# Key heads with decays from stored running sums, block transposes on all 128 rows, and an output projection that takes both parts of its input side by side

## The chip, the cores and the metric

The kernel runs on one core of one Trainium2 chip. The core has five engines with an instruction stream each: TensorE (PE in the profile; its weight loads are PEld), VectorE (DVE), ScalarE (ACT), GpSimd (POOL) and SyncE (SP, which here only issues DMAs). The metric is the device time of one launch in microseconds, lower is better. A comparison of two kernels gives the ratio of their times.

## The reference

The program is a trunk of two layers over 256 latent and 256 context tokens with 2048 features, everything in fp32. Layer 0 joins neighbourhood attention and latent attention; layer 1 is a gated DeltaNet in both directions of time; a final RMSNorm ends it. The change lies almost wholly in layer 1. There are 16 key heads, each of which serves two of 32 value heads, chunks of 64 tokens, and two directions with their own log decays `g` and gains `beta`:

```python
def gated_delta_chunked(q, k, v, g, beta, state0):
    gf = jnp.cumsum(gf, axis=-1)                    # within a chunk of 64
    diff = gf[..., :, None] - gf[..., None, :]
    decay = jnp.where(lower, jnp.exp(jnp.where(lower, diff, 0.0)), 0.0)
    kb = kf * bf[..., None]
    lmat = jnp.where(strict, jnp.einsum('bhncd,bhnsd->bhncs', kb, kf) * decay, 0.0)
    rhs = jnp.concatenate([vf * bf[..., None], kb * jnp.exp(gf)[..., None]], axis=-1)
    sol = lax.linalg.triangular_solve(lmat + jnp.eye(CHUNK), rhs, left_side=True, lower=True)
    intra = jnp.where(lower, jnp.einsum('bhncd,bhnsd->bhncs', qf, kf) * decay, 0.0)
    ...
    state, o = lax.scan(step, state0, xs)           # over the chunks, state 128x128

def deltanet_out(o, z, o_norm, w_out):
    o = rmsnorm(o.transpose(0, 2, 1, 3), o_norm)
    return (o.reshape(b, t_len, DN_MIX_WIDTH) * jax.nn.silu(z)) @ w_out
```

For each chunk, direction and value head there is thus a 64x64 table of decays (exponentials of differences of running sums), a lower triangular system with that table times the products of keys, and a table of query-key products times the decays. `w_out` is 4096 x 2048.

## The kernel before, in words

**Matmuls in three parts.** TensorE multiplies a rounded fp32 format, so each weight tile of 128x1024 is loaded (`raw`, L71, 4 buffers), rounded by ACT into `whi` (L77) and the remainder taken by DVE as `wlo` (L78, 3 buffers each). The activations are split alike into `hh` and `hl`. `dense` (L85 to L93) issues three matmuls for each 128 rows of the weight: `whi`·`hh` (L90), `whi`·`hl` (L91), `wlo`·`hh` (L92), with 512 columns for all tokens and 256 for the latent ones alone. `mm_tile` gives their PSUM tile, of which there are two. The projections of layer 1 to keys, queries, values and gates take their input from such a pair; before it, in layer 0, the same two buffers (tags `hh` and `hl`) hold `ch` with `qr`, and then `gh` with `gl`, the parts of the gated attention output.

**Key heads.** `head(kh)` (L679) runs 16 times. It projects K and Q, convolves them over time on DVE with SiLU on ACT (L557 to L580), transposes the keys on PE to `ptk` (L689), and writes keys and queries into `sp`. Then it makes the decays (L716 to L725) in three goes: forward for all four pairs of chunks, backward for all four, and backward once more, transposed, for two. In each, GpSimd multiplies the decays `ghl` of each token by a mask `incl` into `rhs` (L720, once for the rounded part, once for the remainder), PE sums with a triangular matrix `seg` (L722) into the PSUM tile `pd`, and ACT takes the exponential into `DT`. Four by four small matmuls make the products `kk` of keys with keys and with queries (L736). DVE writes `NT` (decay times key products, L744) and, through a masked copy `QKm` (L740), `AT` (decay times query products, L746). `sp` is stored to DRAM in `spk` and `spt`.

**Inverses.** `inverse(sg)` (L752) runs eight times, each for two key heads, and inverts the triangular 64x64 blocks, 64 of them side by side. Their 32x32 diagonal blocks are gathered by a block transpose into `L` (L764, one for each half of the 128 rows, since the block lies in columns 0 to 31 of the upper half's rows and in 32 to 63 of the lower's). Thirty-one steps of forward substitution follow, two DVE instructions each (L778 `outer`, L780 `X`). GpSimd scales `X` (L782; the last time DVE does). Four block transposes on 64 rows write `X` and its transpose into `U` (L785, L787). Then PE makes the off-diagonal block with small matmuls (`px` L798, `pu` L815), ACT copies it into `U` (L819), and `by_chunk` (L587) stores `U` with eight DMAs from SP. The PSUM tiles `pd`, `px` and `pu` share the tag `xu`.

**What sets the order.** `woven` writes the heads three pieces at a time, each head's first pieces ahead of the last of the one before. The first two heads come alone. Then 42 turns each write seven pieces of an inverse, one of a head, and now and then one of `zunits` (L826, the gates of one head). The 42 turns hold heads 2 to 15 and inverses 0 to 6. Behind them, inverse 7 is written among the last gates and the values of head 0. Up to here, what each engine does in which order is worked out ahead from that text by the builder's scheduler and its own cost estimates; at run time each engine goes through its list in order and waits on semaphores. SP has one list of DMAs: a DMA that waits, for instance for its buffer to be read, holds up those behind it.

**Loop and end.** From L1167 on, an order written out by hand for PE, DVE and ACT runs the recurrence over 64 chunk steps, with value projections between them and, when those are used up, `early` (L1151), which does the first 24 of 32 weight blocks of eight output tiles. `gate` (L1135) splits the gated outputs into `gh` and `gl`, which lie where `hh` and `hl` were. Behind the loop, L1264 to L1271 do the rest of the output projection: eight tiles with 8 blocks and eight with 32, 256 columns each. `project` (L613) adds a tile to the residual stream in two halves. The final norm and the stores end the program.

Of the kernel before, what the change touches and what calls it, by code (L numbers as in the profile page):

```python
# [26 lines left out]
def trunk_kernel(ctx: ExitStack, tc: tile.TileContext, g):  # L27
# [57 lines left out]
    def dense(ps, w, off, kt, xh, xl, k0=0, sl=slice(0, T), first=True, last=True):  # L85
# [7 lines left out]
        return end.ins  # L93

# [136 lines left out]
    hh = big.tile([128, KT, T], F32R, name="hh", tag="hh")  # L231
    hl = big.tile([128, KT, T], F32R, name="hl", tag="hl")
# [69 lines left out]
    with tc.tile_pool(name="ab", bufs=2, reuse_waits="tile") as tp, \  # L302
# [142 lines left out]
        ch = big.tile([128, KT, T], F32R, name="ch", tag="hh")  # L445
        qr = big.tile([128, KT, T], F32R, name="qr", tag="hl")
# [33 lines left out]
        gh = big.tile([128, KT, T], F32R, name="gh", tag="hh")  # L480
        gl = big.tile([128, KT, T], F32R, name="gl", tag="hl")
# [24 lines left out]
        hh = big.tile([128, KT, T], F32R, name="hh", tag="hh")  # L506
        hl = big.tile([128, KT, T], F32R, name="hl", tag="hl")
# [18 lines left out]
    incl = dcst("incl", [128, 3, 64], g["dnc"][:, 1152:1344].rearrange("p (a n) -> p a n", a=3))  # L526
    seg = dnp.tile([128, 3, 128], F32R, name="seg", tag="seg")
# [11 lines left out]
    god = scratch("god", [128, 28, S])  # L539

# [72 lines left out]
    def project(u, p):  # L613

        for t in range(2):
            x = x_of[u].rearrange("p (c i) -> p c i", c=4)[:, pair(t)]
            V.scalar_tensor_tensor(x, p[:, t * 128:t * 128 + 128].rearrange("p (h i) -> p h i", h=2),
                                   mods[1][:, 32 + u, 0:1], x, op0=ALU.mult, op1=ALU.add)


    with tc.tile_pool(name="dn", bufs=2, reuse_waits="tile") as tp, \
# [10 lines left out]
        ch = tp.tile([128, 1792], F32, name="cumh", tag="sp", bufs=1)[:, :1152].rearrange("p (a n) -> p a n", a=9)  # L632
        nc.sync.dma_start(ch, g["dnc"][:, 0:1152].rearrange("p (a n) -> p a n", a=9))
        cum, rest, hones = ch[:, 0:2], ch[:, 2:4], ch[:, 4:6]
        A.copy(seg, ch[:, 6:9])
# [25 lines left out]
        ghl = [tp.tile([128, 2, 128], F32R, name=f"ghl{i}", tag=f"ghl{i}", bufs=1) for i in range(2)]  # L661
        A.copy(ghl[0], gfl)
        V.tensor_tensor(ghl[1], gfl, ghl[0].bitcast(F32), op=ALU.subtract)
# [15 lines left out]
        def head(kh):  # L679
# [4 lines left out]
            yield  # L684

# [29 lines left out]
            for d, c, n in ((0, 0, 4), (1, 2, 4), (1, 1, 2)):  # L715
                pd = ps.tile([128, 512], F32, name="pd", tag="xu")[:, :128 * n]  # L716
                for i in range(2):
                    rhs = tp.tile([128, 8, 64], F32R, name="rhs", tag="rhs")[:, :2 * n]
# [33 lines left out]
        def inverse(sg):  # L752
# [68 lines left out]
            for d in range(2):  # L821
                by_chunk(spu[sg][:, d], U[:, d, 16 * d:16 * d + 16])
# [565 lines left out]
```

## Time and profile before

| | |
|---|---|
| time, median of 3 runs | 2547.64 us (2542.07 to 2549.25) |
| profiled execution, its time | 2550.65 us |
| profiled execution, span of the core | 2548.9 us |
| mean granted clock of TensorE | 0.985 |
| bytes moved by DMA | 394.30 MB, mean 155 GB/s |
| share of the chain that ended last | PE 74%, DVE 12%, issue 6%, DMA 4%, ACT 3% |

The trace falls into stretches: 

| us from the start | what runs there | PE busy | DVE busy | granted clock |
|---|---|---|---|---|
| 0 to 800 | modulation, projections and attention of layer 0 | 770.99 | 481.29 | 1.00 |
| 800 to 1100 | output projection of layer 0, modulation of layer 1 | 293.46 | 226.20 | 0.98 |
| 1100 to 1160 | start of layer 1, first key heads | 54.27 | 32.70 | 1.00 |
| 1160 to 1660 | key heads with inverses 0 to 6 | 460.69 | 479.45 | 0.96 |
| 1660 to 1760 | last gates, inverse 7, values of head 0 | 93.77 | 87.87 | 0.95 |
| 1760 to 2430 | loop over the chunks, `early` towards its end | 667.17 | 482.13 | 1.00 |
| 2430 to 2549 | output projection and final norm | 108 | 64 | 1.00 until 2540 |

All numbers but the first row come from one execution that the hardware profiler took. In the rows of a profile, `L778 DVE SCALAR_TENSOR_TENSOR outer<-L,bv,X 128x255` is an instruction of line 778 on DVE that writes tile `outer` from `L`, `bv` and `X`, 128 partitions by 255 elements; `x201` counts such instructions. Busy time of PE includes stretches in which the clock is throttled: the granted clock says to what share.

### The profile page before, as it was taken

How to read it: one execution, taken by the hardware profiler on the slowest of the kernel's cores; microseconds unless marked ns; L12 is line 12 of the kernel's file. 1: busy time of each engine (PE TensorE's matmuls, PEld its weight loads, DVE VectorE, ACT ScalarE, POOL GpSimd, SP SyncE). 2: the span in 40 equal slices, each digit the busy share in tenths (PEclk: the TensorE clock that was granted, in tenths of full speed). 3: DMA queues.
4: the chain of work that ended last, by engine and by line, in shares of the span. 5: the costliest groups of instructions: out<-in, count | busy, mean ns of one | idle time of the engine just before them, and what ended most of it. 6: DMA issues, size and time to landing. Idle time of an engine off the chain costs nothing.

```text
span 2548.9 us, 43398 instructions
## 1 busy us (share of the span) xinstructions
PE 2448.6 (96%) x16586; PEld 2002.5 (79%) x16586; DVE 1853.5 (73%) x3547; ACT 1140.4 (45%) x2468; POOL 275.6 (11%) x261
## 2 busy tenths in 40 slices
PE   6999999999999999999999989899999999999998
PEld 4557888888768778768888888797777777778898
DVE  4644788873456688758999999997777777777654
ACT  4223323233344422377656665543444444445443
POOL 0000000000000000033322332300000000003000
PEclk9999999999999999999999999999999999999999
DMA  8872645532253367645454544573233333335454
GB/s 251 285 267 83 199 163 172 180 127 91 71 198 112 112 216 225 222 155 160 140 167 148 172 145 156 163 211 104 87 107 110 113 103 105 112 93 180 152 188 141
DMA packets 201809, 394.30 MB, mean 155 GB/s; under 512 B 68224, under 2 KB 109696, under 8 KB 201472
## 3 DMA queue, kind: packets, MB, share of 16 engines
q1 hardware_dynamic: 200448, 389.98, 48.7%
q8 instruction: 131, 2.15, 0.3%
q10 hardware_dynamic: 1152, 1.54, 0.2%
q14 instruction: 78, 0.64, 0.1%
HBM read 356.28 MB, written 35.13 MB: 154 GB/s over the span
## 4 chain that ended last, share of the span: by engine, by line
PE 74%; DVE 12%; issue 6%; DMA 4%; ACT 3%; POOL 0%; SPq 0%; DVEq 0%; POOLq 0%; ACTq 0%
PE mm L90 19%; PE mm L91 17%; PE mm L92 17%; PE pks L993 3%; PE pmod L127 3%; DVE wlo L78 3%; PE ptr L1005 2%; DVE acc L566 2%; PE sp L348 2%; DVE outer L778 1%; PE po L348 1%; DVE X L780 1%; DMA mraw<-dn_wm 1%; DVE U L787 1%; PE ptr L1038 1%
## 5 line engine op out<-in xcount | busy, mean ns | idle before, releaser
L90 PE MATMUL mm<-hh,whi 128*128 128x512 f32 (+1 forms) x2784 | 987.0, 355 | 2.4 <-ACT t L643 2.3
L92 PE MATMUL mm<-hh,wlo 128*128 128x512 f32 (+1 forms) x2784 | 959.3, 345 | 12.2 <-DVE wlo L78 11.5
L91 PE MATMUL mm<-hl,whi 128*128 128x512 f32 (+1 forms) x2784 | 959.7, 345 | 0.0
L77 ACT CAST whi<-raw 128x1024 fp32r<-128x1024 f32 (+2 forms) x346 | 337.6, 980 | 650.5 <-PE mm L91 521.4
L90 PEld LDWEIGHTS mm<-hh,whi 128*128 128x128 f32 x2784 | 534.1, 192 | 112.6 <-issue 33.3
L92 PEld LDWEIGHTS mm<-hh,wlo 128*128 128x128 f32 x2784 | 533.2, 192 | 77.1 <-DVE wlo L78 13.1
L91 PEld LDWEIGHTS mm<-hl,whi 128*128 128x128 f32 x2784 | 534.4, 192 | 62.5 <-issue 9.7
L78 DVE TENSOR_TENSOR wlo<-raw,whi 128x1024 fp32r<-128x1024 f32 (+2 forms) x346 | 400.6, 1160 | 204.0 <-ACT whi L77 201.4
L163 DVE SCALAR_TENSOR_TENSOR lacc<-mraw,cond,lacc 128x512 f32<-128x512 f32 x300 | 208.3, 744 | 0.0
L566 DVE SCALAR_TENSOR_TENSOR acc<-cin,taps,acc 128x508 f32<-128x508 f32 (+3 forms) x256 | 191.9, 750 | 7.6 <-ACT acc L557 5.2
L1015 DVE SCALAR_TENSOR_TENSOR vl<-ptr,egm,vh 128x128 fp32r<-128x128 f32 x224 | 64.6, 346 | 98.2 <-ACT rf L1012 39.3
L720 POOL TENSOR_TENSOR rhs<-ghl,incl 128x512 fp32r<-128x512 f32 (+1 forms) x96 | 113.1, 1193 | 186.6 <-PE pd L722 165.9
L778 DVE SCALAR_TENSOR_TENSOR outer<-L,bv,X 128x31 f32<-128x31 f32 (+15 forms) x248 | 118.1, 476 | 5.1
L127 PE MATMUL pmod<-mraw,cond 128*32 128x512 f32 (+2 forms) x640 | 95.6, 504 | 26.4 <-DMA mraw<-ab_wm 19.1
L1099 DVE TENSOR_TENSOR wlo<-raw,whi 128x1024 fp32r<-128x1024 f32 x84 | 102.5, 1220 | 14.0 <-ACT whi L1091 13.4
L194 POOL TENSOR_TENSOR rs<-ms,half 128x4 f32<-128x4 f32 (+1 forms) x5 | 4.7, 949 | 978.6 <-DVE ms L192 978.6
L580 ACT ACTIVATE ac<-acc 128x128 f32<-128x128 f32 x160 | 37.4, 300 | 153.2 <-DVE acc L566 153.1
L780 DVE TENSOR_TENSOR X<-X,outer 128x31 f32<-128x31 f32 (+15 forms) x248 | 101.1, 408 | 4.9
L90 PE MATMUL mm<-gh,whi 128*128 128x512 f32 x256 | 100.4, 394 | 1.7 <-DVE x1B L498 1.7
L91 PE MATMUL mm<-gl,whi 128*128 128x512 f32 x256 | 100.6, 393 | 0.2 <-DVE gl L486 0.2
L92 PE MATMUL mm<-gh,wlo 128*128 128x512 f32 x256 | 100.1, 392 | 0.0
L1009 ACT ACTIVATE vh<-ptr,egm 128x128 fp32r<-128x128 f32 x224 | 71.2, 374 | 60.7 <-PE ptr L1005 58.9
(290 smaller groups left out, 3562.7 us busy)
## 6 DMA issues: line engine op xcount, KB each, us to landing
raw<-dn_w SPq DMA_DIRECT2D x194, 512.0 KB, 4.1
mraw<-dn_wm SPq DMA_DIRECT2D x96, 512.0 KB, 4.7
mraw<-ab_wm SPq DMA_DIRECT2D x88, 512.0 KB, 5.7
raw<-ab_w SPq DMA_DIRECT2D x66, 512.0 KB, 3.8
raw<-dn_wo SPq DMA_DIRECT2D x64, 512.0 KB, 3.7
raw<-ab_wo SPq DMA_DIRECT2D x32, 512.0 KB, 4.8
raw<-ab_w SPq DMA_DIRECT2D x32, 256.0 KB, 3.5
spt<-sp SPq DMA_DIRECT2D x64, 128.0 KB, 2.2
```

Source lines behind the costliest of these rows:

```text
L77: A.copy(hi[:, :m], raw[:, :m])
L78: V.tensor_tensor(lo[:, :m], raw[:, :m], hi[:, :m].bitcast(F32), op=ALU.subtract)
L90: PE.matmul(ps, wh[:, c], xh[:, k0 + k, sl], start=first and k == 0, stop=False)
L91: PE.matmul(ps, wh[:, c], xl[:, k0 + k, sl], start=False, stop=False)
L92: end = PE.matmul(ps, wl[:, c], xh[:, k0 + k, sl], start=False, stop=last and k == kt - 1)
L127: PE.matmul(pmod[32 * q:32 * q + 32, :m], cond[:, 4 * kg + q, :], raw[c // 1024][:, half + c % 1024:half + c % 1024 + m], start=kg == 0, s ...
L163: V.scalar_tensor_tensor(acc[:, s], raw[:, q], cond[:, k, s:s + 1], acc[:, s], op0=ALU.mult, op1=ALU.add)
L566: V.scalar_tensor_tensor(o3[:, :, i0:i1], p3[:, :, i0 + d:i1 + d], taps[:, ch, t:t + 1], o3[:, :, i0:i1], op0=ALU.mult, op1=ALU.add)
L720: P.tensor_tensor(rhs, ghl[i].bitcast(F32)[:, d, kh * 8:kh * 8 + 2 * n].unsqueeze(2).broadcast_to(sh), incl[:, c].unsqueeze(1).broadcast_t ...
L778: V.scalar_tensor_tensor(o, L[:, rows, k:k + 1].broadcast_to([128, n, m]), bv[:, k:k + 1], X[:, k:k + 1, cols].broadcast_to([128, n, m]), ...
L780: V.tensor_tensor(X[:, rows, cols], X[:, rows, cols], o, op=ALU.subtract)
L1099: V.tensor_tensor(w, raws[j], h.bitcast(F32), op=ALU.subtract)
```

## The change

It does four things.

1. **One tile for both parts.** `hh` and `hl` become one tile `hx` with both parts next to each other (`parts_tile`, tag `hx`); so do `ch` with `qr`, and `gh` with `gl`.
2. **Output projection.** A new `dense2` multiplies `whi` with both parts in one matmul of 512 columns, whose two halves of the PSUM tile stay apart, and `wlo` with the rounded part in one of 256. `project` adds both halves to the residual stream: four additions for a tile where there were two. The last tile keeps `dense`.
3. **Decays.** Ahead of the heads, PE makes the running sums of all log decays once (`pgt`), ACT and DVE split them, and they go to DRAM (`sums`). For each head, `load_sums` brings them back with six DMAs in two layouts: `gcol` with the sums as rows over the columns of `pd`, and `grow` with minus signs to be met in `gcol`, so that one matmul gives differences of sums. `pd` is then a mask `side` (0 or -1e30, by the identity `idr`) plus that product: two matmuls as before, with no product on GpSimd. The exponential of the third go has scale -1. Masked entries of the decays are zero now, so `QKm` goes, and `AT` is made from `kk` in PSUM.
4. **Transposes.** A DMA moves the lower rows' diagonal blocks of `NT` to columns 0 to 31, where nothing is read any more. One block transpose on 128 rows makes `L`, after three pieces of other text, and two make `U`. In `U` the halves of the columns change places, so that storing it takes twelve DMAs instead of eight: eight of them move 128-byte pieces.

The core of the diff:

```diff
+    def dense2(ps, w, off, kt, x, k0=0, first=True, last=True):
+        p2 = ps.rearrange("p (c s) -> p c s", c=2)
+        for k in range(kt):
+            c = off + k * 128
+            wh, wl = w[c // 1024]
+            c = slice(c % 1024, c % 1024 + 128)
+            start, stop = first and k == 0, last and k == kt - 1
+            if stop:
+                PE.matmul(p2[:, 0], wl[:, c], x[:, 0, k0 + k], start=False, stop=False)
+            PE.matmul(p2, wh[:, c], x[:, :, k0 + k], start=start, stop=stop)
+            if not stop:
+                PE.matmul(p2[:, 0], wl[:, c], x[:, 0, k0 + k], start=False, stop=False)
...
-    hh = big.tile([128, KT, T], F32R, name="hh", tag="hh")
-    hl = big.tile([128, KT, T], F32R, name="hl", tag="hl")
+    def parts_tile(name):
+        return big.tile([128, 2, KT, T], F32R, name=name, tag="hx")
+    hx = parts_tile("hx")
+    hh, hl = hx[:, 0], hx[:, 1]
...
+        pgt = ps.tile([128, 2, 128], F32, name="pgt", tag="ks")
+        for d in range(2):
+            PE.matmul(pgt[:, d], gfl[:, d], cum[:, d], start=True, stop=True)
...
+            nc.sync.dma_start(sums[d], gts[:, d].bitcast(F32).rearrange("p x n -> p (x n)"))
...
+        def load_sums(kh):
+            for d in range(2):
+                src = sums[d][8 * kh:8 * kh + 8]
+                for h in range(2):
+                    nc.sync.dma_start(grow[d][32:48, kh % 2].bitcast(F32).rearrange("r (b h i) -> r h b i", b=2, h=2)[:, h],
+                                      src.rearrange("u (x h b i) -> (u x) h b i", x=2, h=2, b=2)[:, h])
+                nc.sync.dma_start(gcol[d][0:4].bitcast(F32), src.rearrange("u (r i) -> r u i", r=4))
...
             for d, c, n in ((0, 0, 4), (1, 2, 4), (1, 1, 2)):
...
-                for i in range(2):
-                    rhs = tp.tile([128, 8, 64], F32R, name="rhs", tag="rhs")[:, :2 * n]
-                    sh = [128, 2 * n, 64]
-                    P.tensor_tensor(rhs, ghl[i].bitcast(F32)[:, d, kh * 8:kh * 8 + 2 * n].unsqueeze(2).broadcast_to(sh),
-                                    incl[:, c].unsqueeze(1).broadcast_to(sh), op=ALU.mult)
-                    PE.matmul(pd, seg[:, c], rhs.rearrange("p u i -> p (u i)"), start=i == 0, stop=i == 1)
+                PE.matmul(pd, idr, side[:, c].unsqueeze(1).broadcast_to([128, 2 * n, 64]), start=True, stop=False)
+                PE.matmul(pd, grow[d][:, kh % 2], gcol[d][:, :2 * n], start=False, stop=True)
...
-            QKm = tp.tile([128, 2, 2, 64], F32, name="QKm", tag="QKm", bufs=1)
...
-                V.tensor_tensor(AT[:, d], DTs[2 * d][:, 0:2], QKm[:, d].unsqueeze(2).broadcast_to([128, 2, 2, 64]),
+                V.tensor_tensor(AT[:, d], DTs[2 * d][:, 0:2], kk[:, 0:2, 64:128].unsqueeze(2).broadcast_to([128, 2, 2, 64]),
...
+            nc.sync.dma_start(NTu[64:128, :, 0:32], NTu[64:128, :, 32:64])
...
-            for b in range(2):
-                r = slice(64 * b, 64 * b + 64)
-                V.transpose(L[r], NTu[r, :, 32 * b:32 * b + 32].rearrange("p u i -> p i u"))
+            for _ in range(3):
                 yield
+            V.transpose(L, NTu[:, :, 0:32].rearrange("p u i -> p i u"))
+            yield
...
-            for b in range(2):
-                r, c = slice(64 * b, 64 * b + 64), slice(32 * b, 32 * b + 32)
-                V.transpose(U[r, 0, :, c].rearrange("p u i -> p i u"), X[r])
-                yield
-                V.transpose(U[r, 1, :, c].rearrange("p u j -> p j u"), X[r].rearrange("p i j -> p j i"))
-                yield
+            V.transpose(U[:, 1, :, 0:32].rearrange("p u j -> p j u"), X.rearrange("p i j -> p j i"))
+            yield
+            V.transpose(U[:, 0, :, 0:32].rearrange("p u i -> p i u"), X)
+            yield
```

The lists of instructions show three places. The first is DVE where the first inverse ends and the second begins, in the stretch of the key heads. Before:

```order
L780 TENSOR_TENSOR X<-X,outer 128x2x30
L778 SCALAR_TENSOR_TENSOR outer<-L,bv,X 128x31
L780 TENSOR_TENSOR X<-X,outer 128x31
L764 STREAM_TRANSPOSE L<-NT 64x1024 x2
L785 STREAM_TRANSPOSE U<-X 64x32x32
L787 STREAM_TRANSPOSE U<-X 64x32x32
L785 STREAM_TRANSPOSE U<-X 64x32x32
L787 STREAM_TRANSPOSE U<-X 64x32x32
L771 STREAM_TRANSPOSE bv<-bt 128x32
L78 TENSOR_TENSOR wlo<-raw,whi 128x1024
```

And of the changed kernel, whose lines have other numbers (L816 and L818 are the substitution, L802 makes `L`, L821 and L823 make `U`):

```order
L816 SCALAR_TENSOR_TENSOR outer<-L,bv,X 128x31
L78 TENSOR_TENSOR wlo<-raw,whi 128x1024
L818 TENSOR_TENSOR X<-X,outer 128x31
L802 STREAM_TRANSPOSE L<-NT 128x1024
L821 STREAM_TRANSPOSE U<-X 128x32x32
L823 STREAM_TRANSPOSE U<-X 128x32x32
L809 STREAM_TRANSPOSE bv<-bt 128x32
L78 TENSOR_TENSOR wlo<-raw,whi 128x1024
```

Six block transposes have become three, at the same place; the transpose into `L` stands directly ahead of those into `U`, as it did.

The second place is SP's list between the stores of key heads 1 and 2 (`spk` and `spt` are stores of a head, `raw` are weight tiles). Before:

```order
L749 DMA spk_8917<-sp 128x768
L71 DMA raw<-dn_w 128x1024 x3
L591 DMA spt_8933<-sp 32x1024 x4
L71 DMA raw<-dn_w 128x1024
L749 DMA spk_8918<-sp 128x768
```

And of the changed kernel, with the loads of the sums, and the move inside `NT` for the first inverse (L797):

```order
L705 DMA gcol_9080<-sums_8968 4x8x64
L703 DMA grow_9082<-sums_8968 16x2x32 x2
L71 DMA raw<-dn_w 128x1024
L705 DMA gcol_9081<-sums_8969 4x8x64
L703 DMA grow_9083<-sums_8969 16x2x32 x2
L71 DMA raw<-dn_w 128x1024 x2
L797 DMA NT<-NT 64x32x32
L610 DMA spt_8928<-sp 32x1024 x4
L71 DMA raw<-dn_w 128x1024
L785 DMA spk_8913<-sp 128x768
```

Seven small transfers now stand between the weight tiles of one head, and those into `gcol` write a buffer that the head before still reads.

The third place is PE's list where `early` begins, between two steps of the recurrence (`ptr`, `pks`). Before:

```order
L1038 MATMUL ptr<-rh,rc 128x128 x2
L993 MATMUL pks<-St,rg 64x256 x4
L993 MATMUL pks<-St,kq_17017 64x256 x2
L90 MATMUL mm<-hh,whi 128x256
L91 MATMUL mm<-hl,whi 128x256
L92 MATMUL mm<-hh,wlo 128x256
```

And of the changed kernel:

```order
L1078 MATMUL ptr<-rh,rc 128x128 x2
L1033 MATMUL pks<-St,rg 64x256 x4
L1033 MATMUL pks<-St,kq_16903 64x256 x2
L105 MATMUL mm<-hx,whi 128x512
L107 MATMUL mm<-hx,wlo 128x256
```

Three matmuls of 256 columns have become one of 512 and one of 256; the steps of the recurrence around them stand where they stood.

More of the change, by code (lines that the diff above doesn't have):

```diff
@@ L479, in trunk_kernel @@
         pace = 0
[L480 to L481 removed]
+        gx = parts_tile("gx")
+        gh, gl = gx[:, 0], gx[:, 1]
         for k in range(KT):
@@ L539, in trunk_kernel @@
     god = scratch("god", [128, 28, S])
+    sums = [scratch(f"sums{d}", [128, 256]) for d in range(2)]
     def dunit(u, sl):
@@ L737, in head @@
                                   tile_position=(0, r.start))
-            QKm = tp.tile([128, 2, 2, 64], F32, name="QKm", tag="QKm", bufs=1)
-            for d in range(2):
-                V.tensor_tensor(QKm[:, d], kk[:, 0:2, 64:128], incl[:, d].unsqueeze(1).broadcast_to([128, 2, 64]),
-                                op=ALU.mult)
             for d in range(2):
```

83 lines of the change are left out of this document (54 added, 29 removed).

## The prediction

> **What bounds the kernel now.** I read the page's first part, then the table of stretches for the stage that changes, then who waits for whom on PE, then the groups of DVE. The page:
>
> ```profile
> PE 2448.6 (96%) x16586; PEld 2002.5 (79%) x16586; DVE 1853.5 (73%) x3547; ACT 1140.4 (45%) x2468; POOL 275.6 (11%) x261
> ```
>
> PE is the busiest over the whole span, but that is an average. The stretches (length, busy time of PE, PEld, DVE, ACT, POOL, then granted clock, DMA share, GB/s) show where it isn't so:
>
> ```profile
> 800.00:1100.00 300.00, 293.46 (x1434) 231.71 (x1433) 226.20 (x413) 109.73 (x227) 12.64 (x10) 0.98 0.57 184
> 1100.00:1160.00 60.00, 54.27 (x327) 43.00 (x323) 32.70 (x54) 43.71 (x98) 20.00 (x20) 1.00 0.46 145
> 1160.00:1660.00 500.00, 460.69 (x4719) 418.89 (x4720) 479.45 (x783) 311.39 (x601) 148.38 (x147) 0.96 0.52 158
> 1660.00:1760.00 100.00, 93.77 (x1037) 83.73 (x1037) 87.87 (x148) 41.61 (x79) 9.44 (x11) 0.95 0.56 162
> 2430.00:2540.00 110.00, 107.54 (x897) 107.39 (x896) 58.88 (x85) 50.54 (x69) 2.51 (x2) 1.00 0.50 157
> ```
>
> From 1160 to 1660 (the key heads with the inverses) DVE is busy 479 of 500 us and PE 461: **DVE sets the pace and PE runs close behind**. PE loses 39 us there to idling, and a mean clock of 0.96 loses another 500 × 0.04 = 20 us. At full clock its work is about 461 − 20 = **441 us**: no change on DVE alone can bring these 500 us below that. In the last row, the output projection, PE is busy 108 of 110 at clock 1.00 and DVE 59: PE alone is the bound.
>
> PE's waits inside 1160 to 1660 (who <- for whom: us, times, longest) add up to those 39 us:
>
> ```profile
> PE pd L722 <- ACT U L819: 10.8, 4, 2.8
> PE mm L92 <- DVE wlo L78: 9.4, 6, 2.6
> PE ptk L689 <- ACT ac L577: 8.7, 3, 3.6
> PE px L798 <- DVE U L787: 4.9, 4, 2.5
> PE pd L722 <- POOL rhs L720: 3.8, 1, 3.8
> ```
>
> Most lead back to DVE: `wlo` is its subtraction, `ac` follows its convolution taps, `U` its transposes.
>
> **The change, part by part: DVE.** The groups of DVE in that stretch, then POOL's largest (count | busy us, mean ns | idle before):
>
> ```profile
> L78 DVE TENSOR_TENSOR wlo<-raw,whi 128x1024 fp32r<-128x1024 f32 x105 | 134.1, 1278 | 11.0 <-ACT whi L77 10.0 <-PE mm L91 0.7
> L778 DVE SCALAR_TENSOR_TENSOR outer<-L,bv,X 128x255 f32<-128x255 f32 (+15 forms) x201 | 99.3, 494 | 3.9
> L780 DVE TENSOR_TENSOR X<-X,outer 128x255 f32<-128x255 f32 (+15 forms) x201 | 85.0, 423 | 3.7
> L764 DVE STREAM_TRANSPOSE L<-NT 64x1024 f32<-64x1024 f32 x14 | 28.6, 2039 | 0.1
> L787 DVE STREAM_TRANSPOSE U<-X 64x1024 f32<-64x1024 f32 x12 | 26.1, 2171 | 0.0
> L785 DVE STREAM_TRANSPOSE U<-X 64x1024 f32<-64x1024 f32 x12 | 23.6, 1964 | 0.3
> L740 DVE TENSOR_TENSOR QKm<-kk,incl 128x128 f32<-128x128 f32 x28 | 6.8, 278 | 0.0
> ...
> L720 POOL TENSOR_TENSOR rhs<-ghl,incl 128x512 fp32r<-128x512 f32 (+1 forms) x88 | 101.8, 1171 | 160.2 <-PE pd L722 159.9
> ```
>
> Transposes: each pair of 64-row ones becomes one of 128 rows. Whether that one costs as much as one half is not in the trace, but other operations show what rows cost:
>
> ```profile
> L341 DVE TENSOR_TENSOR qr<-rope,qr x8: 683/686/690, 717.7 to 738.1; 64x512 fp32r<-64x512 f32 x8
> ...
> L341 DVE TENSOR_TENSOR kT<-mm,kT 128x512 fp32r<-128x512 f32 x16 | 10.9, 683 | 0.0
> ```
>
> 64 and 128 rows take the same 0.68 us, so I take 2.0 to 2.2 us for a whole transpose (bounds: half of the pair, or all of it). Half of 28.6 + 26.1 + 23.6 goes: **39 us**. `QKm` goes too: **7 us**; the product behind it now reads PSUM, as the product for `NT` beside it does already, and I price that at nothing (bounds ±1 us).
>
> POOL: the 88 `rhs` products go. POOL isn't the bound, but DVE is slower beside it. From 1703 to 1740 POOL has no such product, and one whole inverse runs there:
>
> ```profile
> L778 DVE SCALAR_TENSOR_TENSOR outer<-L,bv,X 128x31 f32<-128x31 f32 (+15 forms) x31 | 12.4, 400 | 0.8
> L780 DVE TENSOR_TENSOR X<-X,outer 128x31 f32<-128x31 f32 (+15 forms) x31 | 10.6, 342 | 0.9
> L78 DVE TENSOR_TENSOR wlo<-raw,whi 128x1024 fp32r<-128x1024 f32 x4 | 4.9, 1217 | 0.0
> ```
>
> The same lines, over the same sixteen shapes, mean 494, 423 and 1278 ns beside POOL. 201 × 94 + 201 × 81 + 105 × 61 ns = **42 us** (bounds: 0 if the two stretches differ for another reason; no more than the 102 us of POOL). So DVE drops from 479 to 479 − 39 − 7 − 42 = 391 us, below PE's 441: **PE becomes the bound** of the stage.
>
> What then remains of its waits? The nearest row is 800 to 1100, where PE leads a DVE that is busy 75%: PE busy 293.5 of 300, clock 0.98, so 441 / 0.978 / 0.98 = 460. Here DVE would be busy about 85%, so I take 464: **−36 us** (bounds 0 and −59).
>
> Behind it, 1660 to 1760: the last inverse ends in four transposes that PE waits for, at a clock that fell.
>
> ```profile
> 1746.70 2.21 PE L798 MATMUL px<-U,NT 32*32 32x32 f32 x128 [2.74 <-DVE U L787]
> ```
>
> Two of about 2 us go, which removes this wait, and some of the lost clock (0.05 of 100 us) with it: **−6 us** (0 to −11).
>
> **Output projection.** Start times of PE, three matmuls with 256 columns, then three with 512:
>
> ```profile
> 2531.39 0.28 PE L90 MATMUL mm<-hh,whi 128*128 128x256 f32 x1
> 2531.51 0.28 PE L91 MATMUL mm<-hl,whi 128*128 128x256 f32 x1
> 2531.63 0.28 PE L92 MATMUL mm<-hh,wlo 128*128 128x256 f32 x1
> ...
> 1742.65 0.40 PE L91 MATMUL mm<-hl,whi 128*128 128x512 f32 x1
> 1742.88 0.39 PE L92 MATMUL mm<-hh,wlo 128*128 128x512 f32 x1
> 1743.12 0.39 PE L90 MATMUL mm<-hh,whi 128*128 128x512 f32 x1
> ```
>
> 256 columns take 0.120 us from start to start, 512 some 0.23 (0.227 in the undisturbed rows of other stages). Three of 256 are 0.360 us; one of 512 and one of 256 are 0.347. That is 0.013 us, 480 times (15 of 16 tiles with 32 steps each): **−6 us** (0 to −6.4). The 30 additional half-tile sums are on DVE at 0.34 us, 10 us that PE's 108 of 110 hides; were they in its way, the last tile would feel it, and that one keeps the old form. The Trainium skill, TensorE: Matmul & The Clock Gate, section "Back-to-back issue gap", speaks against most of this: it gives an isolated gap of columns / 2.4 + 2.5 ns, with which the step goes from 327.5 to 325.0 ns and the sum is an estimated 1.2 us. The trace shows about 13 ns above columns / 2.4 per matmul here, so I keep the rows.
>
> **What is added.** Ahead of head 0 the sums go out to DRAM and back. Each way takes two to three us like the smallest rows of the DMA table, while PE has the first Q unit to do: +1 (0 to +4). `hh` and `hl` become one tile, so in the first layer the casts to `gh` wait until `qr` is last read, as `gl` did already; they then run at 0.31 us each beside PE's 0.68 per step: +1 (0 to +6). The six loads of a head and the shift inside `NT` stand in SP's queue among the weights:
>
> ```profile
> rb<-spu SPq DMA_DIRECT2D x16, 128.0 KB, 3.0
> rb<-spu SPq DMA_DIRECT2D x32, 64.0 KB, 2.6
> ...
> SPq L591 <- DVE U L787: 59.6, 8, 15.9
> ```
>
> Twice the pieces (512 against 256, of 256 bytes) land 0.4 us later. The shift's 2048 pieces would by that land in about 2.6 + 1792 × 0.0016 = 5.4 us, an estimate; behind the last `NT` product stand about 6 us of other DVE work before `L` is wanted. I take nothing for it (0 to 5 us per inverse). The loads of `gcol` wait for PE's last `pd` of the head before, and the weight loads behind them wait with them; but SP stood up to 15.9 us for `U` before, and PE's whole wait for `wlo` was 9.4 us. I take nothing.
>
> Sum: −36 − 6 − 6 + 1 + 1 = −46 us. The profiled execution took 2550.65; that gives 2504. The median of the three runs is 3 us lower, so **2501**.
>
> **Rivals.**
>
> *PE's waits vanish almost wholly* (15%). For it: four of the five waits lead to DVE, which gets nearly a fifth of its time back. Against it: PE works in a fixed order with two PSUM tiles. It gives −50 −10 −6 + 2 = −64, with the 3 us 2484 at its weak end and 2471 at the bounds (−59 −11 −6); point 2478.
>
> *DVE keeps half the pace* (20%). `L` waits for its shift at the head of DVE's in-order queue, 5.4 us in seven inverses: 38 us back on DVE, 429 against 441, about as close as the two stand today. Or 128 rows cost twice, and 39 us stay. Then perhaps −18 in the stage and half of the end: −25, 2523, from 2515 to 2538.
>
> *The change does not show* (5%). The waits on PE's own order (`pd` behind `U`, `ptk` behind `ac`) come back at another place: 2540 to 2555.
>
> *Slower: weights late behind `gcol`* (5%). SP issues in order. If a `gcol` load waits longer than the split weights in hand last (three tiles of eight steps of 0.36 us: 8.6 us), PE stands for a whole load: 4.1 us landing, a cast of 1.05 and a subtraction of 1.2, about 6.4 us. Once in each of 16 heads that is 102 us; less the gain of 46, +56: 2604. Against it is the row on SP above.
> The Trainium skill has a rule on this side: DMA: Bandwidth & Descriptors, section "Specifications", asks for 512 bytes or more for line rate and has smaller writes read and modify. The change makes some 52,000 pieces of 128 or 256 bytes. By that rule the transfers would share in this rival; the trace has no 128-byte stores, so it can't tell yet.
>
> **How the numbers follow.** The forecast, 2485 to 2515, has 55%. Faster by over 0.3% (below 2540; about what a measurement of this kernel can tell) are the forecast and the first two rivals: 0.90. Within it 0.05, slower 0.05. The range 2471 to 2530 holds the forecast, the first rival and most of the second; above it are left the rest of that and the last two, under 2 in 10.
>
> **What would show it.** In the stretch of the key heads DVE's busy share falls below PE's; `outer` and `X` mean about 400 and 342 ns; transposes are 24 of about 2.1 us; the stretch is about 36 us shorter; PE's clock is nearer 0.98. In the projection, PE starts a pair of matmuls every 0.347 us. I am wrong if `L` or a weight load shows idle time of DVE or PE behind DMA, or if PE's idle time stays at 39 us with an idle DVE.

## The result, and the profile after

The changed kernel takes 2490.61 us (median of 4 runs, 2489.66 to 2493.04) against 2548.39 us for the kernel before on the same chip: a ratio of 0.978, 95% interval 0.9763 to 0.9797, or 58 us less. Forecast were 2501 with a range of 2471 to 2530. In the profiled executions the span falls from 2548.9 to 2491.2 us. Where that lies, from the start times of three instructions in both traces:

| stretch | before | after | difference |
|---|---|---|---|
| start to the first key transpose (`ptk`) | 1136.7 | 1137.7 | +1.0 |
| from there to the last state update of the loop (`psu`) | 1273.3 | 1216.6 | -56.7 |
| from there to the last matmul of the output projection | 126.3 | 124.2 | -2.1 |

Almost everything is in the second row. The busy times of the changed kernel, first part of the page:

```profile
PE 2428.2 (97%) x16110; PEld 1963.1 (79%) x16110; DVE 1762.8 (71%) x3538; ACT 1105.6 (44%) x2446; POOL 161.1 (6%) x165
```

The key heads with all eight inverses, from the first `ptk` to the last small matmul of inverse 7. Length, then busy time of PE, PEld, DVE, ACT and POOL, granted clock, DMA share and GB/s; first the kernel before, then in a fence of its own the one after:

```profile
1136.70:1753.20 616.50, 570.29 (x5885) 517.54 (x5885) 578.23 (x950) 369.32 (x722) 167.45 (x167) 0.96 0.52 157
```

```profile
1137.70:1692.30 554.60, 545.29 (x5847) 498.39 (x5845) 476.03 (x890) 327.92 (x685) 57.34 (x74) 0.99 0.66 180
```

DVE, which was busy 94% of the stretch, is busy 86%. PE was busy 570 of 616 us at a clock of 0.96 and is busy 545 of 555 at 0.99. The lengths cannot be subtracted as they are, because inverse 7 now ends earlier in PE's list, with 38 fewer matmuls ahead of it; up to 1701.7 us, with as many as before (5890 against 5885), PE takes 564.0 us, that is 52.5 less. GpSimd and ACT lose work as well; ACT's 41 us are not in the prediction. PE's waits in this stretch after the change, which answer to the five of before:

```profile
PE pu L851 <- issue: 3.8, 3, 2.3
PE mm L91 <- issue: 2.5, 1, 2.5
PE pd L762 <- DMA gcol<-sums: 1.3, 1, 1.3
PE mm L92 <- DVE wlo L78: 0.6, 1, 0.6
PE ptk L733 <- ACT ac L596: 0.5, 1, 0.5
```

The waits for `wlo`, `ac` and `U` are all but gone. DVE's groups in the same stretch (count | busy us, mean ns | idle before):

```profile
L78 DVE TENSOR_TENSOR wlo<-raw,whi 128x1024 fp32r<-128x1024 f32 x125 | 152.6, 1223 | 29.4 <-ACT whi L77 27.0 <-DMA spk<-sp 1.1 <-DMA raw<-dn_w 0.7
L816 DVE SCALAR_TENSOR_TENSOR outer<-L,bv,X 128x31 f32<-128x31 f32 (+15 forms) x248 | 99.4, 401 | 6.4 <-POOL X L811 0.5
L818 DVE TENSOR_TENSOR X<-X,outer 128x31 f32<-128x31 f32 (+15 forms) x248 | 84.6, 341 | 5.5
L585 DVE SCALAR_TENSOR_TENSOR acc<-cin,taps,acc 128x508 f32<-128x508 f32 (+3 forms) x128 | 82.1, 642 | 0.8
L780 DVE TENSOR_TENSOR NT<-DT,kk 128x512 f32<-128x512 f32 x32 | 21.7, 679 | 1.6 <-PE kk L776 1.6
L821 DVE STREAM_TRANSPOSE U<-X 128x1024 f32<-128x1024 f32 x8 | 16.6, 2080 | 0.1
L802 DVE STREAM_TRANSPOSE L<-NT 128x1024 f32<-128x1024 f32 x8 | 16.2, 2029 | 19.3 <-DMA NT<-NT 19.3
L823 DVE STREAM_TRANSPOSE U<-X 128x1024 f32<-128x1024 f32 x8 | 15.9, 1987 | 0.0
```

A transpose of 128 rows costs what one of 64 rows did. `outer`, `X` and `wlo` are as fast as they were where GpSimd had no products. And DVE stands 19.3 us in front of `L` for the move inside `NT`. PE's waits for DVE (`wlo` 0.6, `U` 0.4) add up to 1.0 us, so little of that reaches PE.

What ACT loses is seen in its groups. Before:

```profile
L725 ACT ACT_TABLE_LOAD x31 | 39.8, 1283 | 0.6
...
L580 ACT ACT_TABLE_LOAD x27 | 34.6, 1283 | 1.0 <-DMA spz<-zt 0.5
...
L577 ACT ACT_TABLE_LOAD x5 | 6.4, 1283 | 13.4 <-DVE acc L566 13.4
```

After:

```profile
L765 ACT ACT_TABLE_LOAD x16 | 20.5, 1283 | 0.3
...
L596 ACT ACT_TABLE_LOAD x9 | 11.5, 1283 | 3.8 <-DVE acc L585 3.6
...
L599 ACT ACT_TABLE_LOAD x8 | 10.3, 1283 | 0.1
```

ACT loads a table each time it goes from SiLU to the exponential or back: 63 times before, 33 times after, 1.28 us each, 38 us less. The cause stands in ACT's list of instructions. Before, a SiLU is put between the second and the third exponential of a head (L725 and L580; 580 and 577 are SiLUs):

```text
L725 ACT_TABLE_LOAD
L725 ACTIVATE DT<-pd 128x512
L77 CAST whi<-raw 128x1024
L725 ACTIVATE DT<-pd 128x512
L77 CAST whi<-raw 128x1024
L580 ACT_TABLE_LOAD
L580 ACTIVATE zt<-mm 128x128 x2
L577 ACTIVATE ac_9814<-acc 128x128 x4
L725 ACT_TABLE_LOAD
L725 ACTIVATE DTo<-pd 128x256
```

After, the three stand together:

```text
L765 ACT_TABLE_LOAD
L765 ACTIVATE DT<-pd 128x512 x2
L77 CAST whi<-raw 128x1024
L765 ACTIVATE DTo<-pd 128x256
L77 CAST whi<-raw 128x1024
L599 ACT_TABLE_LOAD
L599 ACTIVATE zt<-mm 128x128 x2
```

The whole list has 70 table loads before and 40 after. ACT's two lists show that without any run; the prediction goes by the lists of DVE, SP and PE only.

### The profile page after: what moved, and what is told of

The parts are those of the page before. It is cut to its first block, busy times and chain, and to the rows that moved or that the text cites. A ratio compares the mean times of both kernels' runs of the same rounds, so it can differ in the third digit from the quotient of the medians.

```text
span 2491.2 us, 42483 instructions
## 1 busy us (share of the span) xinstructions
PE 2428.2 (97%) x16110; PEld 1963.1 (79%) x16110; DVE 1762.8 (71%) x3538; ACT 1105.6 (44%) x2446; POOL 161.1 (6%) x165
## 2 busy tenths in 40 slices
DMA packets 254940, 397.24 MB, mean 159 GB/s; under 512 B 122257, under 2 KB 163857, under 8 KB 254609
## 3 DMA queue, kind: packets, MB, share of 16 engines
q8 instruction: 127, 2.08, 0.3%
## 4 chain that ended last, share of the span: by engine, by line
PE 88%; issue 5%; DMA 3%; DVE 2%; ACT 1%; SPq 0%; POOL 0%; DVEq 0%; POOLq 0%; ACTq 0%
PE mm L90 21%; PE mm L91 20%; PE mm L92 20%; PE pks L1033 3%; PE pmod L141 3%; PE ptr L1045 2%; PE sp L365 2%; PE mm L105 2%; PE po L365 1%; DMA mraw<-dn_wm 1%; PE ptr L1078 1%; PE psu L1064 1%; PE pks L1064 1%; PE pt L398 1%; PE mm L107 1%
## 5 line engine op out<-in xcount | busy, mean ns | idle before, releaser
L90 PE MATMUL mm<-hx,whi 128*128 128x512 f32 (+1 forms) x2304 | 843.7, 366 | 2.3 <-ACT t L664 2.2
L91 PE MATMUL mm<-hx,whi 128*128 128x512 f32 (+1 forms) x2304 | 820.6, 356 | 2.5 <-issue 2.5
L92 PE MATMUL mm<-hx,wlo 128*128 128x512 f32 (+1 forms) x2304 | 819.4, 356 | 0.6 <-DVE wlo L78 0.6
L78 DVE TENSOR_TENSOR wlo<-raw,whi 128x1024 fp32r<-128x1024 f32 (+2 forms) x346 | 394.3, 1142 | 204.3 <-ACT whi L77 198.2
L90 PEld LDWEIGHTS mm<-hx,whi 128*128 128x128 f32 x2304 | 438.8, 190 | 106.3 <-issue 27.0
L92 PEld LDWEIGHTS mm<-hx,wlo 128*128 128x128 f32 x2304 | 438.6, 190 | 65.1 <-issue 4.2
L91 PEld LDWEIGHTS mm<-hx,whi 128*128 128x128 f32 x2304 | 438.8, 190 | 61.4 <-issue 9.2
L105 PE MATMUL mm<-hx,whi 128*128 128x512 f32 x480 | 173.1, 404 | 0.1
L107 PE MATMUL mm<-hx,wlo 128*128 128x256 f32 x457 | 128.4, 281 | 1.3 <-DVE wlo L1139 1.2
L105 PEld LDWEIGHTS mm<-hx,whi 128*128 128x128 f32 x480 | 88.9, 188 | 24.5 <-issue 5.0
L816 DVE SCALAR_TENSOR_TENSOR outer<-L,bv,X 128x31 f32<-128x31 f32 (+15 forms) x248 | 99.4, 401 | 6.4 <-POOL X L811 0.5
L90 PE MATMUL mm<-gx,whi 128*128 128x512 f32 x256 | 100.3, 394 | 3.4 <-DVE x1B L515 2.4
L91 PE MATMUL mm<-gx,whi 128*128 128x512 f32 x256 | 100.4, 392 | 0.5 <-DVE gx L503 0.5
L92 PE MATMUL mm<-gx,wlo 128*128 128x512 f32 x256 | 99.8, 391 | 0.0
```

Of the source, the lines that this page charges most:

```text
L78: V.tensor_tensor(lo[:, :m], raw[:, :m], hi[:, :m].bitcast(F32), op=ALU.subtract)
L90: PE.matmul(ps, wh[:, c], xh[:, k0 + k, sl], start=first and k == 0, stop=False)
L91: PE.matmul(ps, wh[:, c], xl[:, k0 + k, sl], start=False, stop=False)
L92: end = PE.matmul(ps, wl[:, c], xh[:, k0 + k, sl], start=False, stop=last and k == kt - 1)
L105: PE.matmul(p2, wh[:, c], x[:, :, k0 + k], start=start, stop=stop)
L107: PE.matmul(p2[:, 0], wl[:, c], x[:, 0, k0 + k], start=False, stop=False)
```

## The experiments

Theory at the start: DVE set the pace and PE does now, so PE's own work is a floor, and any part that takes enough off DVE gains nearly everything (saturation). Rivals: each part gains in proportion to the DVE time it frees (shares); or something else than DVE's time decides.

### The parts one at a time

**side_by_side** is the kernel before with `parts_tile` and `dense2` alone, **decays** with the stored sums alone, **transposes** with the 128-row transposes alone; the diffs are those parts of the change.

> The kernel before with the first two parts of the change alone (one tile for both parts, output projection side by side). By the rows of the trace, a step of 256 + 256 + 256 columns at 0.360 us becomes one of 512 + 256 at 0.347, 480 times: 6 us less than before, a time of about 2542. The key heads (first key transpose to first pks) stay at 616 us. Rival: only the gap between matmuls goes, 1.2 us, and the time is 2547.

> The kernel before with the third part alone (decays from stored sums, no products on GpSimd, no QKm). Saturation theory: the key heads take the longer of two things, PE's own 564 us and DVE's work at 94% busy. DVE drops from 578 by 8 (QKm) and 42 (other engines' contention gone) to 528, which at 94% is 562: the part alone gives nearly all of the gain in this stretch, 46 to 52 us, a time of 2497 to 2503; outer and X mean about 400 and 341 ns. Rival, shares: each part gives a share of the 52 us in proportion to the DVE time that it frees (50 of 100): 26 us, a time of 2522. Rival, no contention: outer stays at 476 ns, only QKm's 8 us are gained.

> The kernel before with the fourth part alone (block transposes on 128 rows, the move inside NT, the stores in 128-byte pieces); GpSimd keeps its products. Saturation theory: 24 transposes of 2.04 us in place of 48, DVE drops from 578 to 529, the key heads fall to PE's 564 to 570 us, a time of 2497 to 2505; outer stays near 476 ns. Rival, shares: half of the 52 us, 2522.

Measured ratios to the kernel before: side_by_side 0.9992 (0.9982 to 1.0001, 2548.89 us), decays 0.9812 (0.9795 to 0.9828, 2504.36 us), transposes 0.9905 (0.9887 to 0.9924, 2527.67 us). In us at 2548: 2, 48 and 24. The interval of side_by_side goes up to a gain of 4.6 us and takes in none at all: it rules out the 6 us expected, not the rival of 1.2. In decays `outer` and `X` mean 400 and 341 ns, and in transposes, where GpSimd keeps its products, 458 and 405: the rival without contention is out. The key heads in the stretches table, decays first:

```profile
1137.90:1711.70 573.80, 555.24 (x5883) 505.04 (x5882) 518.89 (x918) 338.16 (x697) 57.44 (x75) 0.99 0.55 170
```

Transposes alone:

```profile
1132.90:1721.10 588.20, 554.93 (x5844) 503.71 (x5845) 530.76 (x921) 366.83 (x716) 167.32 (x166) 0.98 0.60 169
```

Both take about as much off DVE (59 and 47 us), and the saturation theory has them equal. The first gains twice what the second does. Decays came out at the floor and fits saturation, transposes came out at the shares, and neither theory holds for both. What differs is ACT (338 against 367 us; 46 table loads against 70) and GpSimd (57 against 167): something in the third part counts beside DVE's own time. Three waits of PE in transposes show where:

```profile
PE mm L92 <- DVE wlo L78: 9.5, 6, 2.3
PE ptk L689 <- ACT ac L577: 8.9, 5, 3.6
PE pd L722 <- POOL rhs L720: 4.7, 4, 3.2
```

They are about as long as before (11.5, 8.7 and 4.5 us). In decays the wait for `ac` is 1.5 us. The wait for `U` (10.8 us of PE's `pd` behind it before) shrinks in both.

### The costs put back one at a time

**pool_idle** puts products on GpSimd back into the changed kernel, after the last value that GpSimd makes for a head (160 of them, 130 us of GpSimd, where the kernel before had 96 with 113 us):

```diff
+                for i in range(n):
+                    idle = tp.tile([128, 4, 64], F32R, name="idle", tag="QKm", bufs=1)
+                    P.tensor_tensor(idle, knorm[:, kh].unsqueeze(2).broadcast_to([128, 4, 64]),
+                                    side[:, c].bitcast(F32).unsqueeze(1).broadcast_to([128, 4, 64]), op=ALU.mult)
```

> The changed kernel, with GpSimd products of the same number of elements put back for each head; nobody reads what they write. If other instructions on GpSimd slow DVE, outer rises from 401 to about 476 ns and X from 341 to about 408, and DVE's busy time in the key heads from 478 by about 40 us to some 520. Saturation theory: PE still sets the pace, so the time rises by no more than 6 us, to at most 2497. Rival, shares: 42 of 100 us of DVE's cost 22 us, 2513. If the means stay at 401 and 341, the faster outer has another reason than GpSimd.

0.9834 (0.9811 to 0.9857), 2510.31 us: 14 us slower by the ratios (0.9834 against 0.9780), more than the 6 us that saturation allows. DVE's groups and the stretch:

```profile
L78 DVE TENSOR_TENSOR wlo<-raw,whi 128x1024 fp32r<-128x1024 f32 x124 | 156.8, 1267 | 22.1 <-ACT whi L77 21.7
L820 DVE SCALAR_TENSOR_TENSOR outer<-L,bv,X 128x31 f32<-128x31 f32 (+15 forms) x248 | 108.2, 436 | 5.9 <-POOL X L815 0.2
L822 DVE TENSOR_TENSOR X<-X,outer 128x31 f32<-128x31 f32 (+15 forms) x248 | 94.0, 379 | 5.5
L585 DVE SCALAR_TENSOR_TENSOR acc<-cin,taps,acc 128x508 f32<-128x508 f32 (+3 forms) x128 | 92.2, 720 | 0.8
L784 DVE TENSOR_TENSOR NT<-DT,kk 128x512 f32<-128x512 f32 x32 | 21.7, 679 | 1.1 <-PE kk L780 1.1
```

```profile
1142.10:1713.90 571.80, 551.58 (x5847) 503.30 (x5845) 509.99 (x889) 327.51 (x685) 189.76 (x234) 0.98 0.63 175
```

Nobody reads these products, and still `outer` goes from 401 to 436 ns, `X` from 341 to 379, the convolution's `acc` from 642 to 720, and DVE's busy time rises by 34 us. Other work on GpSimd does slow DVE, if by less than the 476 and 408 ns of the kernel before. `NT`, which reads one of its inputs from PSUM, stays at 679 ns, and the transposes stay near 2.0 us. The Trainium skill, SBUF — State Buffer, section "SBUF: two separate sides", says which operations contend: the two engines share one pair of ports, and a DVE operation takes it in its two-port modes or when it has two inputs in SBUF, the latter only against a GpSimd operation that reads SBUF; whichever starts first holds the pair for its whole instruction. The trace agrees on which are slowed: `outer`, `X` and `acc`, with two inputs in SBUF, and not `NT` and the transposes.

**trans_twice** issues each block transpose of the changed kernel twice (a `for _ in range(2):` ahead of each). **act_tables** brings ACT's table loads back:

```diff
+                if n == 2:
+                    A.activation(DTs[2][:, 0, 0, 0:1], DTs[1][:, 0, 0, 0:1], AF.Silu)
                 A.activation(DTs[-1].rearrange("p s h i -> p (s h) i"), pd, AF.Exp, ...)
```

> The changed kernel with each of its 24 block transposes issued twice into the same place: 24 times 2.03 us, 49 us more on DVE, which goes from 476 to about 525 in the key heads, with GpSimd and ACT as they are. The theory of saturation has fallen with the transposes alone and the unread products. In its place, theory of slack: each us of DVE's work costs about half a us while PE's order is as tight as this, so about +24 us, a time of 2515. Rival, only the other engines matter: what the third part gained came from ACT and GpSimd, and PE has cover enough for DVE at 525 of 560: at most +8 us, 2499.

> The changed kernel with one small SiLU of 128x1 put between the second and the third exponential of each head (the third then overwrites what it wrote): ACT loads its function tables 70 times as in the kernel before, not 40, that is 30 times 1.28 us = 38 us more on ACT, with DVE and GpSimd as they are. Theory: the table loads stand in front of the copies and SiLUs that DVE and PE wait for, and part of what the third part gains beyond DVE's time (47 us, against 22 of the transposes that free as much of DVE) is theirs: +8 to +20 us, 2499 to 2511. Rival: ACT is busy 328 of 555 us and hides them: at most +3 us, 2494.

trans_twice: 0.9857 (0.984 to 0.9874), 2508.97 us, 20 us slower than the changed kernel: near the 24 us of the theory of slack, and not its rival. act_tables: 0.9835 (0.9816 to 0.9854), 2505.34 us, 14 us slower: the table loads count. Their stretches, trans_twice first:

```profile
1137.30:1714.80 577.50, 557.05 (x5890) 507.53 (x5888) 518.68 (x921) 330.90 (x691) 55.82 (x75) 0.98 0.61 173
```

```profile
1140.30:1698.30 558.00, 543.84 (x5845) 497.46 (x5844) 475.14 (x889) 367.82 (x731) 56.47 (x74) 0.99 0.64 179
```

Each adds work to one engine only: DVE 476 to 519 us, ACT 328 to 368. (The profiled run of act_tables took 2499.26 us and the other three 2505 to 2507, so its stretch shows less than the median does.) PE's longest wait in each, trans_twice, then pool_idle, then act_tables:

```profile
PE px L837 <- DVE U L823: 9.9, 6, 6.4
```

```profile
PE ptk L733 <- ACT ac L596: 7.0, 4, 4.1
```

```profile
PE ptk L733 <- ACT ac L596: 4.5, 3, 2.1
```

In the changed kernel these two waits are 0.4 and 0.5 us. By the ratios, 43 us more of DVE cost 20 us, 34 us more of DVE through GpSimd 14 us, and 40 us more of ACT 14 us. The engine that got the work is busy 90, 89 and 66% of its stretch, always less than PE, and still the time rises. In trans_twice PE is idle 11 us more than in the changed kernel, and 9.5 of them are the one wait for `U`: there the cost is, for the most part, the delay in the chain from an inverse's last step to PE, which the doubled transposes lengthen. That each us of DVE's work costs about half a us, as the theory of slack has it, is therefore not shown by it.

**all_three** puts the three together.

> The changed kernel with all three costs put back at once: the unread GpSimd products, every block transpose twice, and the small SiLU that brings ACT's table loads back to 70. Against the changed kernel at a ratio of 0.9780, they cost 0.0054, 0.0077 and 0.0055 by themselves. If the account is complete and the costs add, the ratio is 0.9966, about 2540, and DVE is again busy over 93% of the key heads. Rival, they overlap as the parts do when taken away (48 and 24 us alone, 54 together): three quarters, 0.992, about 2527.

0.9992 (0.9982 to 1.0001), 2546.31 us: the gain is gone. Against the changed kernel that is 54 us, where the three costs by themselves add up to 47; so they do not overlap. DVE is busy 92% of the key heads, where over 93 were expected. **after_again**, on the same chip:

> The changed kernel as it is, beside the other two on one chip: a ratio of 0.978 again, between 0.976 and 0.980.

0.9782 (0.9768 to 0.9797), 2490.99 us. One line keeps all_three from being the kernel before over again; it is PE's longest wait:

```profile
PE px L843 <- DVE U L829: 27.9, 6, 6.4
```

Before, that wait was 7.9 us, and others were longer. Here the doubled transposes stand in the chain from the last step of an inverse to PE. So the size comes back, though the masked copy `QKm` does not; but PE stands at another place, and that the costs act as they did in the kernel before is not shown.

### The one tile and the output projection

> The changed kernel without its first two parts: three matmuls of 256 columns in the output projection, and two tiles for the parts. Theory: what side by side gains (a pair of matmuls 0.352 against 0.360, 480 times, 4 us) the one tile gives back in layer 0 (3.5 us), so no more than 2 us slower than the changed kernel. Rival, the 6 us of the first estimate: 6 us slower, if the one tile costs nothing.

**no_side** is the kernel before with the third and fourth part: 0.9782 (0.9762 to 0.9802), 2489.31 us. The first two parts bring nothing that can be measured, alone (0.9992) or with the others. The pairs of the changed kernel's output projection, by start times on PE:

```profile
2439.61 0.40 PE L105 MATMUL mm<-hx,whi 128*128 128x512 f32 x1
2439.85 0.28 PE L107 MATMUL mm<-hx,wlo 128*128 128x256 f32 x1
2439.97 0.40 PE L105 MATMUL mm<-hx,whi 128*128 128x512 f32 x1
2440.21 0.28 PE L107 MATMUL mm<-hx,wlo 128*128 128x256 f32 x1
2440.32 0.40 PE L105 MATMUL mm<-hx,whi 128*128 128x512 f32 x1
```

0.36, 0.35: over the undisturbed pairs of this kernel the mean is 0.352, against 0.360 for three of 256 columns, so 0.0077 us 480 times, 3.7 us. Layer 0 takes some of it back. Some 250 matmuls there, from 673 us on, took 63.3 us before and 62.8 in no_side, but 63.8, 67.3 and 66.8 in the changed kernel, in after_again and in side_by_side. The stretch and PE's largest wait in it, before:

```profile
673.40:736.70 63.30, 56.03 (x252) 36.05 (x251) 30.77 (x58) 29.08 (x47) 0.00 (x0) 0.97 0.51 171
...
PE pmod L127 <- DMA mraw<-dn_wm: 3.2, 5, 1.4
```

In after_again:

```profile
673.60:740.90 67.30, 58.04 (x252) 35.10 (x251) 29.61 (x56) 29.30 (x47) 0.00 (x0) 0.95 0.49 160
...
PE pmod L141 <- DMA mraw<-dn_wm: 7.9, 4, 3.5
```

PE waits longer for the modulation weights there, in the changed kernel itself 6.1 us with only 0.5 us lost, in others up to 7.9 with 4 lost. These are single profiled executions, and the changed kernel's own keeps most of what the pairs give; so the balance of the two parts is not settled closer than the intervals. Why these loads come later with one tile stays open. **gx_in_place** looked for the loss elsewhere, at the casts of `gh`, which with one tile wait for both halves:

```diff
-        gx = parts_tile("gx")
-        gh, gl = gx[:, 0], gx[:, 1]
+        gx = cx
+        gh, gl = ch, qr
```

> The changed kernel, with the parts of the gated attention output in layer 0 written into the tile that holds ch and qr, each half as soon as its own readers are done, and not into a new tile that waits for both. From the last attention matmul with qr to the last of the output projection, the kernels with the new tile take 191 us and those without 187. Theory: the one tile costs these 3.5 us; they come back, 2487. Rival: noise between launches, 2490 to 2491.

0.9785 (0.9766 to 0.9804), 2492.21 us: no gain. The 191 against 187 us on which that theory stood came from a last attention matmul that stands at another place in the list; from 742 us to the end of that projection it is 323.0 us before and 323.5 after. The loss is earlier, as shown above.

### Two tries at a faster kernel

**both** adds to gx_in_place that the move inside `NT` is issued in `head`, behind the products:

```diff
+            for d in range(2):
+                nt = NTs[sg][64:128, d, k2].rearrange("p s h i -> p (s h) i")
+                nc.sync.dma_start(nt[:, :, 0:32], nt[:, :, 32:64])
```

> gx_in_place, and the move inside NT issued for each head right behind its products and not at the start of the inverse. DVE's 19 us of waiting for that move go. Theory of slack: DVE idle behind the move costs like work, a half of it: 9 us less than gx_in_place, 2478. Rival: the wait is hidden, at most 2 us less than gx_in_place.

0.9795 (0.9777 to 0.9813), 2494.95 us: no gain. But the edit did not take the wait away: DVE stands in front of `L` for 17.1 us in gx_in_place and for 16.0 here, 11.8 of them for the moves and 4.2 for a store (`spt`). So this run does not test whether the wait is hidden. That rests on the changed kernel's trace, in which PE hardly waits for DVE.

**q_z_side** takes the projections to queries and gates side by side too:

```diff
+        if sl is XS:
+            dense2(p, w, 0, KT, hx, sl=XS)
+            h2 = tp.tile([128, S], F32, name="h2", tag="QKm", bufs=1)
+            A.copy(h2, p[:, S:])
+            V.tensor_tensor(p[:, :S], p[:, :S], h2, op=ALU.add)
+            return p[:, :S]
```

> The changed kernel with the projections to queries and gates (48 units of 16 steps, 256 columns) done side by side as well; ACT copies the second half, DVE adds it in PSUM. PE: 768 steps, 0.008 us less each, 6 us less work. DVE: 48 additions of some 0.41 us, 20 us; ACT: 48 copies, 16 us, and its list has 54 table loads in place of 40, 18 us. By the prices of the three costs put back (0.40 us of time per us of DVE's work, 0.36 per us of ACT's) that is +8 and +12, less 6: 14 us slower than the changed kernel, a ratio of 0.984. Rival, PE alone sets the pace of the key heads now: 6 us faster, 0.976.

0.979 (0.9767 to 0.9814), 2495.42 us: about the changed kernel's time, between the two expectations. The additions cost 0.43 us each and ACT has 47 table loads in the stretch (54 in its list), about as foreseen, but the prices per us of the three costs put back did not carry over. No kernel tried is measurably faster than the changed one.

## Why the prediction was right, and where not

**DVE sets the pace, PE close behind.** Half right. Two of the three costs run through DVE's time, but the longer of two busy times is not what sets the pace: 34 to 43 us more on an engine that is then busy 66 to 90%, less than PE, cost 14 to 20 us. Saturation, the idea behind the forecast's 464 us, fell with transposes and pool_idle; for the changed kernel itself it holds, with PE busy 98%.

**Transposes: 39 us off DVE.** Right: 1.99 to 2.08 us for 128 rows, at the lower bound, and over all eight inverses 98.5 us become 48.7.

**QKm: 7 us, the product behind it at nothing.** Right. The 7.8 us of the whole stretch are gone, and the products for `AT` take 0.41 us, no more than before.

**GpSimd beside DVE: 42 us.** Right in mechanism and size: `outer` 401 ns (forecast 400), `X` 341 (342), `wlo` 1223 (1217), together 41.5 us over the whole stretch, where 42 were forecast for 500 us of it, and pool_idle and decays show that GpSimd is the cause.

**PE becomes the bound, 464 us for 441.** Right in the mechanism, short in its size: 42 us were forecast for the two stretches, and the second row of the table, less 1.5 us for 192 pairs in the loop, gives 55. The sum took the loss of 5% from a stretch in layer 0 with DVE at 75%. Measured is 545.3 us of PE at clock 0.99 in 554.6, about 540 of full-clock work, so a loss of under 3%. The clock took part: before, 0.96 in 616 us; after, 0.99. The first rival, waits that vanish, had this part right; the time lies between the points of the two, in the forecast's own range. The 13 us by which the sum is short are about the 14 us that act_tables finds for ACT's table loads, a term that the sum does not have: with the loads put back the kernel gains 42 us in all, where 46 were forecast. Whether the 5% would have been right without them was not tried apart.

**What the prediction missed.** Thirty table loads of ACT, 38 us: 24 of them go with the third part alone (decays has 46 loads), none with the fourth (transposes has 70). That the exponentials come together because GpSimd's products no longer stand between them is read from the order worked out ahead, not tried. act_tables prices the thirty at 14 us. With GpSimd's slowing of DVE (14 us by pool_idle) they make up at most 28 of the 48 us that the third part alone gains; they are a reason why it gains more than the fourth, and the rest was not taken apart.

**Output projection, -6 us.** Mis-sized: a pair takes 0.352 us and not 0.347, so 3.7 us, since 512 columns beside 256 start 0.232 apart and not 0.227. The rule that the prediction weighs, by which 1.2 us would go, is as far from it on the other side. The one tile in layer 0, priced at 1 us with a bound of 6, takes back 0.5 to 4 us in single traces, at another place than the casts it was priced for: both parts together bring 2 us alone, not clear of none, and nothing that shows with the others.

**Added work.** Right for the time, wrong for the move inside `NT`, which was priced at nothing because 6 us of other work would cover its 5.4. It came late: DVE stood for it up to 7.1 us, six times, 19.3 us in all. Idle time of DVE at `L` behind a DMA is one of the signs by which the prediction calls itself wrong, and it showed; but with PE waiting 1.0 us for DVE in the whole stretch, and idle for 9, it can have cost only a few us. No run takes this wait away alone. The slower rival, weights late behind `gcol`, did not come; SP stood there, PE did not:

```profile
SPq L705 <- PE pd L761: 29.4, 10, 4.1
SPq L705 <- PE pd L762: 21.7, 10, 2.7
```

51 us of SP, while PE's whole wait for `wlo` is 0.6 us. And the transfers of 128 and 256 bytes (packets under 512 bytes go from 68224 to 122257) go with a DMA share of the stretch of 0.66, where it was 0.52 and the shorter stretch alone would make it 0.58. PE waits once behind them, 1.3 us for `gcol`: the rule on small transfers that the prediction names decided nothing here.

## What to carry to other kernels

When two engines run at 93% beside each other in a fixed order, do not look for the one bound: price each cost by putting it back alone, and check that all of them together give the old time and the old waits. Such a price belongs to the place where the work stands, as q_z_side shows, and not to each us of an engine. Before a prediction, compare the lists of every engine, ACT's table loads above all, because a change on GpSimd or DVE can regroup exponentials and SiLUs without touching them. A second engine on the same memory ports is paid for by DVE even when its own results are never late.

## What was not expected of the hardware

A block transpose of 128 rows by 1024 columns takes 2.0 us, the same as one of 64 rows (1.96 to 2.16 in the kernel before), as the prediction took from other operations. In the run with transposes alone one of the three took 2.31; why is open. A table load is 1.283 us every time. The Trainium skill, ScalarE: Activation LUTs, section "What ACT_TABLE_LOAD costs", adds a drain of about 1.38 us to each; here a load began 0.02 us after the SiLUs ahead of it, and the exponential behind it 0.01 us after its end, so no such drain shows:

```profile
1300.08 0.91 ACT L577 ACTIVATE ac<-acc 128x128 f32<-128x128 f32 x4
1301.01 1.28 ACT L725 ACT_TABLE_LOAD   x1
1302.30 0.38 ACT L725 ACTIVATE DTo<-pd 128x256 f32<-128x256 f32 x1
```

That is the kernel before, at 1301 us. The granted clock of PE was 0.96 in the key heads with 46 us of idle time and 0.99 with 9, but 0.94 with 41 in all_three, so it does not go by the idle time alone; the cause was not tried.
